# The opening of a decoder block's input projection: three plain units on un-normalised operands

## The chip, the core and the metric

The kernel runs on one core of one Trainium2 chip. The core has five engines with a queue each: TensorE (PE; its weight loads, PEld, run beside its matmuls), VectorE (DVE), ScalarE (ACT), GpSimd (POOL) and SyncE (SP), which here issues all DMAs. The metric is the time of one execution in microseconds on the device; lower is better.

## What is computed

One layer of a decoder with two mixers side by side. Sequence 2048, model width 1024, all in float32.

```
h    = rmsnorm(x, norm1_g)                  # per position: x / rms(x) * gain
proj = h @ w_in                             # 1024 -> 3088: q, k, v, g, a, conv B, C, H
o    = rmsnorm(gla(q, k, v, a)) * silu(g)   # gated linear attention, 4 heads, chunked
conv = B * causal_conv3(C * H)
x    = x + concat(o, conv) @ w_out
h2   = rmsnorm(x, norm2_g)
x    = x + (silu(h2 @ w_gate) * (h2 @ w_up)) @ w_down
return rmsnorm(x, norm_f_g)
```

The change touches the first two lines: the norm of x, and the first columns of the projection (k, q and half of v).

## The kernel before

**Products in three passes.** A float32 operand is split into a high and a low part: ACT copies it to the matmul's reduced format (L163), DVE subtracts that from the original (L164). A product is three matmuls of 128x128 by 128x512: high by high, and high by low both ways.

**Blocks and units.** The 2048 positions are four blocks of 512, j = 0..3; a half is two blocks. Activations lie with features on the partitions: x of one block is eight slices of 128 features, k = 0..7 (input `xt`); `x` has the same numbers by rows. A unit is 256 output columns for a half, its weights four quarters of 128x512: A11, A12, A22, A21. The operands of a half are the quarters B11 (k 0 to 3, first block), B12 (k 0 to 3, second block), B21, B22 (k 4 to 7). A *plain* unit has all eight quarter products, 96 matmuls. Every other unit (`unit`) makes seven products of sums of quarters, 84 matmuls; the weights' sums S1 to S4 are made on POOL (L430 to L437), the operands' differences T1 to T4 for a half once, and each is then split. Its products are, in order, A11.B11, S1.T1, S2.T2, A12.B21, S3.T3, S4.B22, A22.T4.

**The opening.** Units 0 and 1 of half 0 are plain, 2 to 11 are not. `first_loads` loads the rows of block 0 in half rows, unit 0's weights, the rows of block 1 and the slices of block 1. ACT squares the rows with a running sum (L595, L565), and TensorE transposes the rows of block 0 into slices, 32 transposes (L599). `rows_rstd` (L540) makes the factor 1/rms of each position, spreads it over partitions by copies (L552) and turns it by four transposes (L555). `build_first` (L322) multiplies each slice by gain and factor (L615), splits it and gives it to unit 0 (L362 to L364), first all of block 0, then block 1. `plain_unit` (L385) is unit 1; the differences T1 to T4 are made from the normalised slices (L374).

**What sets the order.** Instructions are issued to the engines by a planner that takes them by priority, in the order in which they are written, as soon as its own clock finds them ready. `issue_after` puts an instruction behind another on its engine. Buffers limit how far ahead work may run: four weight buffers (`wqp`), 28 operand buffers (`opp`), eight banks of results, eleven work tiles ("b"). Beside the units runs a list of background steps; `tick` (L241), called after each product, takes one step, at each call while `hurry` is set and at every second one else. In half 0 it holds the gate's weights, a pause of 8 steps, the gate of half 0 (32 matmuls L702, four L724, then four forget gates in tile g) taken in turn with the squares of blocks 2 and 3 (`row_stats`, half rows), and `h1_ahead`, which makes the operands of half 1.

Of the kernel before, what the change touches and what calls it, by code (L numbers as in the profile page):

```python
# [10 lines left out]
F32 = mybir.dt.float32  # L11
# [41 lines left out]
def tile_hymba_block(ctx, tc, x, xt, win, wa, wgu, wout, wffn, wdown, wdown_first, small, out):  # L53
# [98 lines left out]
    second_weights, unit_splits, unsplit = [], [], []  # L152
# [8 lines left out]

    def split(src, hi, lo):
        last_hi[:] = [act.activation(hi, src, AF.Copy)]  # L163
        last_lo[:] = [dve.tensor_tensor(lo, src, hi.bitcast(F32), ALU.subtract)]  # L164
        return last_lo[0]
# [94 lines left out]

    def pause(n):
        for _ in range(n):
            yield
# [58 lines left out]
    def build_first(quad, w):  # L322


        ops = {b: [] for _, b in PRODUCTS}
        h, o = {}, {}
        quarters = ("A11", "A12"), ("A21", "A22")
        los = []

        def weight(n, i, *marks):  # L330
            with ExitStack() as stack:
                for m in (last_exp[0], *marks):
                    stack.enter_context(tc.issue_after(m.ins))
                w[n] = weight_quarter(first_raw[0][:, i, :])

        weight("A11", 0, last_copy[0])
        los.append(last_lo[0])
        for j in range(2):
            for r in range(2):
                o[r, j] = bank()  # L340
            for k in range(KD):
                with tc.issue_after(los[-2 if len(los) > 2 else -1].ins):
                    h[k, j] = quad(k, j)
                if (j, k) == (0, 0):
                    weight("A21", 3, last_scaled[0])
                x = opp.tile([P, 2, PB], F32R, name="op", tag="op")
                los.append(split(h[k, j][:], x[:, 0, :], x[:, 1, :]))
                hi = last_hi[0]
                if j == 0 and k in (1, 2):
                    weight(*(("A12", 1), ("A22", 2))[k - 1], los[-1])  # L350
# [5 lines left out]
                name = ("B11", "B12")[j] if k < 4 else ("B21", "B22")[j]  # L356
                ops.setdefault(name, []).append(x)
                c = slice(k % 4 * P, (k % 4 + 1) * P)
                for r in range(2):
                    q = w[quarters[r][k // 4]]  # L360
                    with tc.issue_after(last_turn[0].ins):
                        pe.matmul(o[r, j][:], q[:, 0, c], x[:, 0, :], start=k == 0, stop=False)  # L362
                    pe.matmul(o[r, j][:], q[:, 1, c], x[:, 0, :], start=False, stop=False)
                    pe.matmul(o[r, j][:], q[:, 0, c], x[:, 1, :], start=False, stop=k == KD - 1)  # L364

        def differences(wanted):
            for n, y, a, b in (
                ("T1", (0, 0), (0, 1), (0, 0)), ("T2", (0, 0), (4, 1), (0, 0)),
                ("T3", (0, 1), (4, 1), (0, 1)), ("T4", (0, 0), (4, 0), (0, 0)),
            ):  # L370
                for k in range(4 if n in wanted else 0):
                    yy, aa, bb = [h[k + dk, j] for dk, j in (y, a, b)]
                    with tc.issue_after(los[-1].ins):
                        dve.tensor_tensor(yy[:], aa[:], bb[:], ALU.subtract)  # L374
# [142 lines left out]
    def row_stats(b):  # L517
# [11 lines left out]
        for t in range(PT):  # L529
            xs = nxt  # L530
            if t + 1 < PT:
                nxt = fetch(t + 1)
# [855 lines left out]
```

## Time and profile before

| | |
|---|---|
| median of 3 runs | 2062.1 us (2059.88 to 2063.85) |
| span of the profiled execution | 2059.3 us |
| TensorE busy, of the span | 2018.4 us (98%) |
| DVE, ACT, POOL busy | 1425.3, 959.7, 859.8 us |
| first product of unit 0 starts | 16.39 us |
| granted TensorE clock, mean | 0.996 |

The span is from the first to the last instruction of one profiled execution; of that execution no other time is given, and the runs' times hold what lies around the span as well. Times in the profile count from the span's start. A busy TensorE is one that has a matmul in its pipeline. Rows in order of time give start, duration, engine, line, operation, output and inputs, shapes, and in brackets the idle time before them with what ended it. Rows by stretch give, for each engine, busy time and the number of instructions, then the granted clock, the busy share of the DMA engines and GB/s.

### The profile page before, as it was taken

What the parts mean: (1) busy time and instruction counts of PE and PEld (TensorE: products, weight loads), DVE (VectorE), ACT (ScalarE), POOL (GpSimd) and SP (SyncE); (2) the same over time, 40 slices, a digit from 0 to 9 for tenths busy, and PEclk for the clock granted to TensorE, in tenths of its full rate; (3) what the DMA queues carried; (4) which work ended last, traced back from release to release, by engine and by line L of the source; (5) the groups of instructions that cost most, each with busy time, mean ns of one, the idle gap of its engine ahead of it and who ended that gap; (6) DMA issues with size and microseconds to landing.
All of it is one profiled execution on the core that took longest, in us unless ns stands there. A gap on an engine that the chain in (4) does not pass through costs nothing.

```text
span 2059.3 us, 27063 instructions
## 1 busy us (share of the span) xinstructions
PE 2018.4 (98%) x9229; PEld 1657.3 (80%) x9229; DVE 1425.3 (69%) x2128; ACT 959.7 (47%) x1918; POOL 859.8 (42%) x622
## 2 busy tenths in 40 slices
PE   7999999999999999999999999999999999999997
PEld 6877888787888888888888878787888888878786
DVE  8789686559743886676675676767666666667774
ACT  6655365765542344444444452334434444453344
POOL 0345322122102564464564345534644544435544
PEclk9999999999999999999999999999999999999998
DMA  6378485416586873545454676476444434586653
GB/s 229 116 274 278 159 319 165 143 67 194 190 296 246 311 254 130 198 181 207 156 185 143 241 264 254 185 282 257 163 164 167 175 140 169 179 309 223 234 217 126
DMA packets 188729, 421.47 MB, mean 205 GB/s; under 512 B 19792, under 2 KB 65072, under 8 KB 178992
## 3 DMA queue, kind: packets, MB, share of 16 engines
q1 hardware_dynamic: 188592, 419.76, 57.2%
q8 instruction: 72, 1.18, 0.2%
q14 instruction: 65, 0.53, 0.1%
HBM read 274.98 MB, written 144.70 MB: 204 GB/s over the span
## 4 chain that ended last, share of the span: by engine, by line
PE 84%; DVE 7%; DMA 4%; ACT 3%; issue 1%; POOL 1%; SPq 0%; DVEq 0%; ACTq 0%; POOLq 0%
PE mm L448 24%; PE mm L449 23%; PE mm L450 23%; PE mm L945 3%; PE mm L948 3%; PE mm L946 3%; DVE wq L164 2%; DVE op L164 1%; DMA op<-sa_B 1%; DMA op<-sa_T 1%; PE a_ps L702 1%; ACT wq L163 1%; DMA siT<-lo 1%; PE o_ps L869 1%; PE o_ps L871 1%
## 5 line engine op out<-in xcount | busy, mean ns | idle before, releaser
L448 PE MATMUL mm<-op,wq 128*128 128x512 f32 x2499 | 973.7, 392 | 10.3 <-ACT c L480 5.3
L449 PE MATMUL mm<-op,wq 128*128 128x512 f32 x2499 | 972.5, 390 | 1.6 <-DVE op L164 1.6
L450 PE MATMUL mm<-op,wq 128*128 128x512 f32 x2499 | 961.3, 390 | 2.6 <-DVE wq L164 2.3
L164 DVE TENSOR_TENSOR wq<-raw,wq 128x512 fp32r<-128x512 f32 (+2 forms) x626 | 508.9, 818 | 262.6 <-ACT wq L163 260.0
L163 ACT ACTIVATE wq<-raw 128x512 fp32r<-128x512 f32 (+2 forms) x626 | 364.9, 589 | 585.6 <-PE mm L450 447.9
L448 PEld LDWEIGHTS mm<-op,wq 128*128 128x128 f32 x2499 | 468.9, 188 | 114.9 <-ACT c L480 8.0
L450 PEld LDWEIGHTS mm<-op,wq 128*128 128x128 f32 x2499 | 469.1, 188 | 103.8 <-DVE wq L164 6.1
L449 PEld LDWEIGHTS mm<-op,wq 128*128 128x128 f32 x2499 | 469.3, 188 | 99.1 <-DVE op L164 3.7
L432 POOL TENSOR_TENSOR raw<-s,raw 128x512 f32<-128x512 f32 (+2 forms) x97 | 133.3, 1374 | 518.5 <-DVE wq L164 474.7
L430 POOL TENSOR_TENSOR s<-raw 128x512 f32<-128x512 f32 (+2 forms) x97 | 127.4, 1313 | 247.5 <-DMA raw<-in_wffn_dram 90.7
L473 DVE TENSOR_TENSOR c<-mm,c 128x512 f32<-128x512 f32 x198 | 135.8, 686 | 72.7 <-PE mm L450 70.9
L473 DVE TENSOR_TENSOR y<-mm,y 128x512 f32<-128x512 f32 x185 | 126.9, 687 | 83.3 <-PE mm L450 82.9
L437 POOL TENSOR_TENSOR raw<-raw 128x512 f32<-128x512 f32 (+2 forms) x97 | 120.6, 1244 | 126.7 <-DVE wq L164 126.7
L927 POOL TENSOR_TENSOR ssx<-ssx,q 128x512 f32<-128x512 f32 x52 | 77.4, 1504 | 158.8 <-ACT q L926 158.5
L431 POOL TENSOR_TENSOR raw<-raw 128x512 f32<-128x512 f32 (+2 forms) x97 | 137.3, 1416 | 4.9
L480 ACT ACTIVATE c<-mm 128x512 f32<-128x512 f32 x198 | 116.1, 587 | 11.1 <-PE mm L450 9.3
L945 PE MATMUL mm<-op,wq 128*128 128x512 f32 x256 | 100.9, 395 | 0.0
L946 PE MATMUL mm<-op,wq 128*128 128x512 f32 x256 | 99.7, 389 | 0.0
L163 ACT ACTIVATE wq<-s 128x512 fp32r<-128x512 f32 (+2 forms) x97 | 56.9, 587 | 89.3 <-PE mm L450 85.4
L164 DVE TENSOR_TENSOR wq<-s,wq 128x512 fp32r<-128x512 f32 (+2 forms) x97 | 82.6, 852 | 2.8 <-ACT wq L163 2.1
L164 DVE TENSOR_TENSOR op<-op 128x512 fp32r<-128x512 f32 x94 | 76.8, 844 | 4.7 <-ACT op L163 4.6
L948 PE MATMUL mm<-op,wq 128*128 128x512 f32 x256 | 79.8, 390 | 0.0
(204 smaller groups left out, 1807.6 us busy)
## 6 DMA issues: line engine op xcount, KB each, us to landing
raw<-in_wffn_dram SPq DMA_DIRECT2D x44, 1024.0 KB, 6.5
sa_B<-so SPq DMA_DIRECT2D x47, 512.0 KB, 4.2
op<-sa_B SPq DMA_DIRECT2D x47, 512.0 KB, 7.1
raw<-in_win_dram SPq DMA_DIRECT2D x23, 1024.0 KB, 5.4
sa_T<-so SPq DMA_DIRECT2D x44, 512.0 KB, 4.5
op<-sa_T SPq DMA_DIRECT2D x44, 512.0 KB, 6.9
raw<-in_wdown_dram SPq DMA_DIRECT2D x24, 768.0 KB, 5.8
sx<-y SPq DMA_DIRECT2D x48, 256.0 KB, 4.0
```

The source lines that it names most:

```text
L163: last_hi[:] = [act.activation(hi, src, AF.Copy)]
L164: last_lo[:] = [dve.tensor_tensor(lo, src, hi.bitcast(F32), ALU.subtract)]
L430: pool.tensor_tensor(s1, a21, a22, ALU.add)
L431: pool.tensor_tensor(a21, a11, a21, ALU.subtract)
L432: pool.tensor_tensor(a11, s1, a11, ALU.subtract)
L448: pe.matmul(o[:], wh, xh, start=first and k == 0, stop=False, skip_group_check=True)
L449: pe.matmul(o[:], wh, xl, start=False, stop=False, skip_group_check=True)
L450: return pe.matmul(o[:], wl, xh, start=False, stop=k == n - 1, skip_group_check=True)
L473: dve.tensor_tensor(t[:], o[:], t[:], ALU.add)
L945: pe.matmul(o[e, j][:], wh, m[:, 0, :], start=k == 0, stop=False)
L946: pe.matmul(o[e, j][:], wh, m[:, 1, :], start=False, stop=False)
L948: pe.matmul(o[e, j][:], wl, ops[k][j][:, 0, :], start=False, stop=k == KD - 1)
```

## The change

Block 0's slices are loaded from `xt` and no longer transposed. The first three units are plain, and their operands are slices with the gain alone; the factor of a position is multiplied onto their results (`out`). The normalised slices (`normed`), B11 to B22 and T1 to T4, serve unit 3 and those after it. All rows, those of blocks 2 and 3 too, are squared in the opening. Twelve matmuls on a tile of ones come first. From there to the weights of unit 3 each ACT and each DVE instruction is put behind the one written before it (`queued`); a low part is held back until the next high part has been issued (`late`, `catch_up`). TensorE's first turn lies behind its product of column (1, 1), its second turn behind the first quarter of unit 1, and the products that follow lie behind the turns. `between` puts the last operands and results among unit 3's weights. The gate is a background step without pause or squares.

Of the diff, its core; inside `opening` the removed lines that a line-by-line comparison puts between the new ones are left out.

```diff
-    second_weights, unit_splits, unsplit = [], [], []
+    unit_splits, unsplit = [], []
...
+    tails, late, ordered = {}, [], []
+
+    def queued(eng, issue):
+
+        with behind([tails[eng]] if eng in tails else []):
+            tails[eng] = issue()
+        return tails[eng]
+
+    def catch_up():
+        while late:
+            last_lo[:] = [queued(dve, late.pop(0))]
+
+    def split_in_order(src, hi, lo, gain=None):
+
+        scale = 1.0 if gain is None else gain
+        last_hi[:] = [queued(act, lambda: act.activation(hi, src, AF.Copy, scale=scale))]
+        catch_up()
+        top = hi.bitcast(F32)
+        if gain is None:
+            late.append(lambda: dve.tensor_tensor(lo, src, top, ALU.subtract))
+        else:
+            late.append(
+                lambda: dve.scalar_tensor_tensor(lo, src, gain, top, ALU.mult, ALU.subtract)
+            )
+
     def split(src, hi, lo):
+        if ordered:
+            return split_in_order(src, hi, lo)
         last_hi[:] = [act.activation(hi, src, AF.Copy)]
         last_lo[:] = [dve.tensor_tensor(lo, src, hi.bitcast(F32), ALU.subtract)]
         return last_lo[0]
...
-    def in_turn(one, *others):
-
-        for other in others:
-            for _ in other:
-                yield
-                if next(one, True) is None:
-                    yield
-        yield from one
-
...
-    def build_first(quad, w):
-
...
-                if j == 0 and k < PT:
-                    with tc.issue_after(hi.ins):
-                        row_squares(k)
-                if (j, k) == (0, PT + 2):
-                    rbs[1] = rows_rstd(squares[1][:, :, 0])
...
-    def plain_unit(src, ops, differences):
-
-        raw = raw_weights(src)
-        us, columns = [], (("B11", "B21"), ("B12", "B22"))
-        w = [weight_quarter(raw[:, i, :]) for i in (0, 1, 3, 2)]
-        second_weights[:] = last_hi + last_lo
-        differences(("T1", "T2", "T3"))
...
-    def unit_weights(src, raw=None):
+    def unit_weights(src, raw=None, between=()):
         raw = raw_weights(src) if raw is None else raw
+        between = iter(between)
+
+        def others():
+            for job in next(between, ()):
+                job()
+
...
         w["S1"] = weight_quarter(s1)
+        others()
         w["S2"] = weight_quarter(a11)
+        others()
         w["A12"] = weight_quarter(a12)
+        others()
         w["S3"] = weight_quarter(a21)
+        others()
         pool.tensor_tensor(a12, a12, a11, ALU.subtract)
         w["S4"] = weight_quarter(a12)
+        others()
         w["A22"] = weight_quarter(a22)
+        others()
         halves.clear()
         return w
 
...
-    def unit(src, ops, into=None, onto=None, raw=None):
-
-
-
-        w = unit_weights(src, raw)
+    def unit(src, ops, into=None, onto=None, raw=None, between=()):
+
+
...
-    def row_stats(b):
-        ssq = mtiny.tile([P, PT, 2], F32, name="ssq", tag="ssq")
-
...
+    def opening():
...
+        warm = bank("warm")
+        for _ in range(12):
+            pe.matmul(warm[:, 0:P], ones[:], ones[:], start=True, stop=True)
+        for what, i in (
+            (fetch_w, 0), (fetch_x, (0, 0)), (fetch_w, 3), (fetch_x, (1, 0)), (fetch_x, (2, 0)),
+            (fetch_w, 1), (fetch_rows, (0, 0)), (fetch_x, (3, 0)), (fetch_w, 2),
+            (fetch_x, (4, 0)), (fetch_rows, (0, 1)), (fetch_x, (5, 0)), (fetch_rows, (0, 2)),
+            (fetch_x, (6, 0)), (fetch_x, (7, 0)), (fetch_x, (0, 1)), (fetch_rows, (0, 3)),
+        ):
+            what(*i) if isinstance(i, tuple) else what(i)
+        for k in range(1, KD):
+            fetch_x(k, 1)
+        raws = {1: raw_weights(win[1])}
         for t in range(PT):
+            fetch_rows(1, t)
+        ordered.append(True)
...
+        def operand(k, j):
+            x = raw_op[k, j] = opp.tile([P, 2, PB], F32R, name="op", tag="op")
+            split_in_order(h[k, j][:], x[:, 0, :], x[:, 1, :], col(C_G1 + k))
+        def square(b, t):
+            if b not in squares:
+                squares[b] = mtiny.tile([P, PT, 2], F32, name="ssq", tag="ssq")
+            r = rows[b, t][:]
+            queued(
+                act,
+                lambda: act.activation(
+                    r, r, AF.Square, accum_out=squares[b][:, t, 0:1]
+                ),
+            )
+        def first_estimate(b):
+            v, l, y = [mtiny.tile([P, PT], F32, name=n, tag=n) for n in ("msq", "rl", "ry")]
+            ssq = squares[b][:, :, 0]
+            queued(
+                dve, lambda: dve.tensor_scalar(v[:], ssq, 1.0 / D, EPS, ALU.mult, ALU.add)
+            )
+            queued(act, lambda: act.activation(l[:], v[:], AF.Ln))
+            queued(act, lambda: act.activation(y[:], l[:], AF.Exp, scale=-0.5))
+            return v, l, y
+        def spread(v, l, y):
+            for f in (
+                lambda: dve.tensor_tensor(l[:], y[:], y[:], ALU.mult),
+                lambda: dve.scalar_tensor_tensor(l[:], l[:], -0.5, v[:], ALU.mult, ALU.mult),
+                lambda: dve.scalar_tensor_tensor(v[:], l[:], 1.5, y[:], ALU.add, ALU.mult),
+            ):
+                queued(dve, f)
+            rep = bt("rep", (P, PT, P))
             for t in range(PT):
+                queued(
+                    dve,
+                    lambda: dve.tensor_copy(
+                        rep[:, t, :], v[:, t : t + 1].to_broadcast([P, P])
...
+        def turn(rep, mark):
+            rb = bank("rb_ps")
+            with behind([mark]):
+                for t in range(PT):
+                    done = pe.transpose(rb[:, t * P : (t + 1) * P], rep[:, t, :], ident[:])
+            return rb, done
+        def keep(b, rb):
+            rbs[b] = bt("rb")
+            queued(act, lambda: act.activation(rbs[b][:], rb[:], AF.Copy))
+        def normed(k, j, rb):
+            y = h[k, j][:]
+            queued(
+                dve,
+                lambda: dve.scalar_tensor_tensor(
+                    y, y, col(C_G1 + k), rb[:], ALU.mult, ALU.mult
+                ),
+            )
+        def out(o, dst, j, r):
+            c = tt("c")
+            queued(dve, lambda: dve.tensor_tensor(c[:], o[:], rbs[j][:], ALU.mult))
+            store(dst[0][j][dst[1] + r][:], c[:])
+        def difference(y, a, b):
...
+        def made(n):
+            for k in range(4):
+                b11, b12, b21, b22 = h[k, 0], h[k, 1], h[k + 4, 0], h[k + 4, 1]
+                y, a, b = {
+                    "B11": (b11, None, None), "B21": (b21, None, None), "B22": (b22, None, None),
+                    "T1": (b11, b12, b11), "T2": (b11, b22, b11), "T3": (b12, b22, b12),
+                    "T4": (b11, b21, b11),
+                }[n]
+                if a is not None:
+                    difference(y, a, b)
+                final(n, k, y)
...
+        def column(k, j):
+            for r in range(2):
+                if k == 0:
+                    o[0, r, j] = bank()
+                q = w[(("A11", "A12"), ("A21", "A22"))[r][k // 4]]
+                last = step3(o[0, r, j], q, k, raw_op[k, j], k == 0, k == KD - 1)
+            return last
...
+        def second(u, j, i):
+            for r in range(2):
+                if i == 0:
+                    o[u, r, j] = bank()
+                q = w[(("A11", "A12"), ("A21", "A22"))[r][i]]
+                for k in range(4 * i, 4 * i + 4):
+                    last = step3(o[u, r, j], q, k, raw_op[k, j], k == 0, k == KD - 1)
+            return last
+        def outs(u, j):
+            for r in range(2):
+                out(o[u, r, j], ((s_kq, 0), (s_kq, 2), (s_v, 0))[u], j, r)
...
+        weight("A11", w_raw[:, 0, :])
+        operand(0, 0)
+        weight("A21", w_raw[:, 3, :])
+        operand(1, 0)
+        operand(2, 0)
+        weight("A12", w_raw[:, 1, :])
+        square(0, 0)
+        operand(3, 0)
+        weight("A22", w_raw[:, 2, :])
+        operand(4, 0)
+        square(0, 1)
+        operand(5, 0)
+        square(0, 2)
+        operand(6, 0)
+        operand(7, 0)
+        operand(0, 1)
+        square(0, 3)
+        catch_up()
+        for k in range(KD):
+            column(k, 0)
+        est = first_estimate(0)
+        operand(1, 1)
+        operand(2, 1)
+        rep = spread(*est)
+        catch_up()
+        for k in range(2):
+            mark = column(k, 1)
+        rb0, turned = turn(rep, mark)
+        for k in range(3, KD):
+            operand(k, 1)
+        catch_up()
+        with behind([turned]):
+            for k in range(2, KD):
+                column(k, 1)
+        weights(1, "A11", "A21")
+        catch_up()
+        keep(0, rb0)
+        for k in range(KD):
+            normed(k, 0, rb0)
+        outs(0, 0)
         for t in range(PT):
+            square(1, t)
+        weights(1, "A12", "A22")
+        for t in range(PT):
+            fetch_rows(2, t)
+        est = first_estimate(1)
+        made("B11")
+        catch_up()
+        rep = spread(*est)
+        rb1, turned = turn(rep, second(1, 0, 0))
+        keep(1, rb1)
+        with behind([turned]):
+            for j, i in ((0, 1), (1, 0), (1, 1)):
+                second(1, j, i)
+        for t in range(PT):
+            square(2, t)
+        raws[2] = raw_weights(win[2])
+        for i in range(6):
+            load(
+                carry[16 * i : 16 * i + 16, 0:2, :],
+                wgu[0:16, :].rearrange("p (h c) -> p h c", c=P),
+            )
+        for t in range(PT):
+            fetch_rows(3, t)
         for k in range(KD):
+            normed(k, 1, rb1)
+        outs(0, 1)
+        made("T1")
+        catch_up()
+        outs(1, 0)
+        weights(2, "A11", "A21")
+        catch_up()
+        for t in range(PT):
+            square(3, t)
+        second(2, 0, 0)
+        weights(2, "A12", "A22")
+        catch_up()
+        outs(1, 1)
+        raw3 = raw_weights(win[3])
+        made("T2")
+        catch_up()
+        for j, i in ((0, 1), (1, 0), (1, 1)):
+            second(2, j, i)
+        made("B21")
+        catch_up()
+        outs(2, 0)
+        made("T3")
+        between = [
+            [],
+            [partial(made, "B22"), partial(outs, 2, 1)],
+            [partial(made, "T4")],
+        ]
+        return ops, raw3, between
...
-    ops, first, differences = build_h()
+    ops, raw, between = opening()
     hurry.append(True)
     background.extend(
         [
-            gate_weights(), pause(8), in_turn(gate(0, ops), row_stats(2), row_stats(3)),
-            unhurried(),
-            h1_ahead(),
+            gate_weights(), gate(0, ops), unhurried(), h1_ahead(),
         ]
     )
-    in_proj(0, ops, first, differences)
+    in_proj(0, ops, raw, between)
     drain_background(lambda: len(background) < 2)
```

More of the change, by code (lines that the diff above doesn't have):

```diff
@@ L2 @@
 from collections import deque
+from functools import partial
 from itertools import chain
@@ L627, in gate_weights @@
         r0, r1 = raw[:, 0:4, 0:16], raw[:, 4:8, 0:16]
-        with behind(second_weights):
+        with behind(unit_splits):
             split(r0, top[:, :, 2, :], top[:, :, 3, :])
```

235 lines of the change are left out of this document (69 added, 166 removed).

## The prediction

> **What bounds the kernel now.** I read the page first, then busy time by stretch, the groups of the first 28 us, and the first 45 us in order of time.
>
> ```profile
> span 2059.3 us, 27063 instructions
> PE 2018.4 (98%) x9229; PEld 1657.3 (80%) x9229; DVE 1425.3 (69%) x2128; ACT 959.7 (47%) x1918; POOL 859.8 (42%) x622
> ...
> PE 84%; DVE 7%; DMA 4%; ACT 3%; issue 1%; POOL 1%; SPq 0%; DVEq 0%; ACTq 0%; POOLq 0%
> ```
>
> TensorE sets the time: it is busy for 98% of the span and holds 84% of the chain that ended last. A change of the opening pays only by what it moves the point at which TensorE has done a given piece of work.
>
> ```profile
> core 0: us, PE busy (x) PEld busy (x) DVE busy (x) ACT busy (x) POOL busy (x), PEclk, DMA share, GB/s
> 0.00:28.30 28.30, 17.06 (x75) 13.96 (x76) 19.27 (x47) 18.98 (x42) 1.11 (x7) 0.94 0.88 315
> 28.30:61.00 32.70, 32.70 (x147) 27.10 (x146) 31.46 (x52) 18.72 (x36) 9.80 (x3) 1.00 0.36 130
> 61.00:110.30 49.30, 49.30 (x218) 40.55 (x217) 34.72 (x66) 32.76 (x74) 13.44 (x9) 1.00 0.40 138
> 110.30:160.00 49.70, 48.43 (x214) 38.69 (x212) 39.44 (x70) 25.64 (x51) 27.83 (x19) 1.00 0.81 284
> 160.00:200.00 40.00, 37.78 (x165) 30.96 (x166) 37.67 (x44) 20.48 (x41) 23.97 (x16) 1.00 0.84 283
> ```
>
> ```profile
> L362 PE MATMUL mm<-op,wq 128*128 128x512 f32 x12 | 5.5, 458 | 2.4 <-ACT op L163 2.4
> L363 PE MATMUL mm<-op,wq 128*128 128x512 f32 x12 | 5.4, 447 | 0.0
> L364 PE MATMUL mm<-op,wq 128*128 128x512 f32 x12 | 4.2, 431 | 0.0
> ```
>
> The first fence is busy time by stretch, the second the TensorE groups of the first 28.3 us. By 28.3 us only 36 products of unit 0 have been started. From there to 110.3 us TensorE has no gap: 147 + 218 entries, less two counted on both sides of a border and three transposes, are 360 products in 82.0 us, 0.228 us each. So the 396 products of units 0 to 3 with the gate (96 + 96 + 84 + 84, and 32 + 4) are through at 110.3 us. I chose this mark because the new kernel has the same work there, plus 12 products.
>
> **The change, step by step.** These are rows of the opening in order of time (start, duration, engine; rows between them are left out).
>
> ```profile
> 4.96 0.63 ACT L595 ACTIVATE q<-xr 128x512 f32<-128x512 f32 x1 [2.89 <-DMA xr<-in_x_dram]
> 7.33 0.63 ACT L595 ACTIVATE q<-xr 128x512 f32<-128x512 f32 x1 [0.94 <-DMA xr<-in_x_dram]
> ...
> 12.75 0.16 DVE L177 SCALAR_TENSOR_TENSOR msq<-rl,ry 128x4 f32<-128x4 f32 x1
> ...
> 16.24 1.04 ACT L565 ACTIVATE xr<-xr 128x1024 f32<-128x1024 f32 x1
> 16.39 0.73 PE L362 MATMUL mm<-op,wq 128*128 128x512 f32 x1 [2.42 <-ACT op L163]
> 16.92 0.63 PE L363 MATMUL mm<-op,wq 128*128 128x512 f32 x1
> 17.18 0.19 ACT L565 ACTIVATION_READ_ACCUMULATOR xr<-xr 128x1 f32 x1
> 17.34 0.63 PE L362 MATMUL mm<-op,wq 128*128 128x512 f32 x1
> ...
> 24.07 0.19 ACT L169 ACTIVATE rl<-msq 128x4 f32<-128x4 f32 x1
> 24.29 0.21 ACT L170 ACTIVATE ry<-rl 128x4 f32<-128x4 f32 x1
> 26.11 0.63 ACT L163 ACTIVATE op<-h 128x512 fp32r<-128x512 f32 x1 [0.62 <-DVE h L615]
> 27.58 0.63 DVE L552 COPY rep<-msq 128x128 f32<-128x128 f32 x4
> 28.35 0.48 PE L362 MATMUL mm<-op,wq 128*128 128x512 f32 x1
> 30.77 1.29 POOL L430 TENSOR_TENSOR s<-raw 128x512 f32<-128x512 f32 x1 [28.96 <-DMA wa<-in_wa_dram]
> 31.35 1.27 DVE L164 TENSOR_TENSOR op<-h,op 128x512 fp32r<-128x512 f32 x1
> 34.24 0.73 DVE L615 SCALAR_TENSOR_TENSOR h<-h,sml,rb_ps 128x512 f32<-128x512 f32 x1
> 34.90 0.68 DVE L164 TENSOR_TENSOR op<-h,op 128x512 fp32r<-128x512 f32 x1
> 35.50 0.74 DVE L615 SCALAR_TENSOR_TENSOR h<-h,sml,rb_ps 128x512 f32<-128x512 f32 x1
> ```
>
> Prices: a two-tensor DVE operation over 512 columns takes its place for 0.60 us (34.90 to 35.50), one with a column factor for 0.66 (34.24 to 34.90), a tiny one 0.16 (12.75), taken as 0.2 since each waits for the one before, the four copies that spread the factors 0.63. On ACT a high part costs 0.63, the logarithm and exponential 0.43 together, a square over 1024 columns 1.04 plus 0.19 for its sum.
>
> *Loads.* Two fine windows give the rate.
>
> ```profile
> 10.00:15.00 5.00, 1.98 (x16) 1.48 (x14) 3.28 (x13) 4.42 (x13) 0.00 (x0) 1.00 1.05 408
> 15.00:20.00 5.00, 3.62 (x9) 2.84 (x10) 4.86 (x8) 3.92 (x8) 0.00 (x0) 0.66 1.03 397
> ```
>
> The first piece of 256 KB is there at 4.96, the third at 7.33; from then on about 400 GB/s, or 0.65 us per piece. In the new order the last slice of the first column, x(7,0), is byte 4.72 million and lands at 7.33 + 3.93/0.40 = 17.2; the last rows of block 0 (5.50 million) at 19.1; unit 1's weights (8.39 million) at 26.3. Block 0's slices are 2 MB more than before, 5.2 us of loading, and SP's queue carries the rows between them: without the 1.57 MB of rows ahead of it x(7,0) would land 3.9 us sooner. Both lie in these landings.
>
> *TensorE until the first turn.* It no longer waits for a normalised operand (16.39 now), nor has it the 32 transposes of x. The second piece lands at about 5.7 (4.96 and 0.65), their high parts 0.63 later: first product near 6.4. The twelve warming products are not in the old trace; they cost nothing while they end by then: from about 1, at most 0.42 each as the slowest products quoted, they end by 6.1. It then follows the slices: x(7,0) at 17.2, its parts 18.5, its products 19.5.
>
> *The ordered DVE queue.* ACT squares the last rows from 19.1 to 20.3; the mean 0.2, logarithm and exponential 0.4: 21.0; high part of x(1,1) 21.6. From there DVE works without a break in the written order: low part of x(1,1) 0.66; three tiny steps and four copies 1.2 (23.5); six low parts 4.0 (27.5); unit 1's A11 and A21 1.2 (28.7); eight norms 5.3 (34.0); two results of unit 0 1.2 (35.2); A12, the mean, A22 1.4, with 0.6 of waiting for ACT (37.2); four low parts of B11 2.4 (39.6); three tiny steps and four copies 1.2: 40.9. A11 and A21 can only be split when unit 0's buffer is free: TensorE has column 1 through k = 3 at 19.5 + 1.4, wait to 22.3, 1.0, transposes to 23.9, 2.7: 26.7; its high part is ready at 27.4, just in time.
>
> *The wait that takes the old one's place.* TensorE ends unit 0 at 26.7 + 5.5 = 32.2 and unit 1's first quarter at 37.7. Everything behind it is tied to the second turn, which needs the copies of 40.9. It stands about 3 us and goes on at 41.0 (the row at 28.35 stands 0.14 behind the copies' end). All else of unit 1 is queued behind it.
>
> *From 41.0 on* there are 72 + 96 + 84 products: 57.4 us, to 98.4; the gate's 36 add 8.2: 106.6. The 12 extra products of the third plain unit (2.7 us) are in this. The nearest cover: unit 2's first weights come on DVE after 41.1 + 5.3 (norms) + 1.2 + 4.8 (T1) + 1.2 + 1.2 = 54.8, wanted at 57.4. S3 comes behind S2, which waits for POOL and a buffer until about 78.6, then 0.6 + 2.4 (B22) + 1.2 + 0.6 + 4.8 (T4) + 0.6 = 88.8, wanted at 79.3 + 4 x 2.73 = 90.2. The extra DVE work (12 results, which ACT copied before, and 12 low parts of B11, B21, B22, 14.4 in all) is hidden only there; its uncovered part is the 3 us.
>
> So 110.3 - 106.6 = **3.7 us gained in the opening**. Bounds: without the wait 3 more; if the loads keep the 0.65 us pace from the first on, 1.1 more (the third piece was that late); with TensorE at half clock 2.6 less (below).
>
> *Behind the opening.* The 16 half-row squares of blocks 2 and 3 leave the background.
>
> ```profile
> PE mm L450 <- DVE wq L164: 1.8, 4, 0.6
> PE mm L448 <- ACT c L480: 1.7, 1, 1.7
> ```
>
> These are TensorE's waits from 110 to 260 us, 3.5 in all, where DVE is busy 37.67 of 40 with blocks 2 and 3's operands. That work can start sooner, with its squares and buffers ready. Ends: all 3.5 gone, or a new wait as in the second rival below; I take 1.0 gone, nearer to nothing, as the DVE and POOL work itself stays.
>
> The sum: -3.7 - 1.0 = -4.7 on the profiled span (2059.3), carried over to the runs' median of 2062.1: **2057.4**. A measurement tells about 0.2% (4.1 us) from no change, so the forecast lies just beyond that.
>
> **Rivals.** *Half clock in the opening, so that the early start buys little.* At 16.92 to 17.34 products stand 0.42 us apart, and the clock is 0.66 in the window from 15, after one in which TensorE was busy 1.98 of 5 us. If the twelve warming products don't hold the clock up and it is half until 19.9 as here, 32 products are done by then; the 40 left to column 1, k = 3, with the turn, end at 29.5, A11's parts wait until 30.2 and the queue slips 2.6: 2060.0. Against: by the landings TensorE's new gaps before 18.5 are short ones, some 3.5 us in 12.
>
> The Trainium skill (TensorE: Matmul & The Clock Gate, Part 1) says that the clock drops to half when a free-running window of about 3.4 us passes idle, and comes back after a busy one. The trace agrees: the half clock follows the emptiest stretch, the two windows quoted with the loads. By that rule the 3 us wait at the second turn would just not drop it; were it over 3.4, one window at 0.42 would lose 1.6 us: 2059.0.
>
> *The gate crowds unit 4.* The pause and the squares between the gate's steps are gone, so all four forget gates are issued within unit 3.
>
> ```profile
> 85.00:114.00 29.00, 15.28 (x28) 9.24 (x20) 1.00 0.61 212
> ```
>
> This row is their tile g on DVE and ACT: 15.3 us on DVE, spread over 29. DVE from 79.2: B22 2.4, two results 1.2, A12 0.6, T4 4.8, S3, S4, A22 1.8, unit 3's sums 1.8, the gate 15.3, unit 4's A11 and S1 1.2, and four POOL sums that each stretch a DVE operation by 0.6 (1.27 at 31.35): 31.5, to 110.7, against 106.6. The wait of 4.1 gives 2062.1 - 3.7 + 4.1 = 2062.5. For it: priority follows the order of issue. Against: the gate waits on ACT in between, and TensorE now loses nothing while it runs (49.30 busy of 49.30).
>
> The Trainium skill (SBUF — State Buffer, SBUF: two separate sides) has POOL and a DVE operation with two SBUF inputs hold a shared port by turns for a whole instruction. The row at 31.35 agrees: 1.27 where 0.68 is usual (34.90). If each of the four held DVE for its full 1.29, the sum would be 2.8 larger: 2065.3.
>
> *Slower.* The same place, with the factors of blocks 2 and 3 ahead of unit 4's weights too, their squares being ready. One set has thirteen tiny steps, 2.6, and its copies:
>
> ```profile
> 124.45 1.74 DVE L552 COPY rep<-ry 128x128 f32<-128x128 f32 x4
> ```
>
> That is 4.3 per set: the wait is 8.4 with one, 12.7 with both: 2066.8 to 2071.1. It decides from a wait of 7.8 on. For it: DVE is the opening's bound already. Against: unit 4's weights can slip in while tiny steps wait.
>
> **How the numbers follow.** The forecast's case 0.60, with a range of its own from 2053 to 2059.5; about 0.50 of it lies below 2058.0 and 0.10 above. Half clock 0.08 and the crowded unit 4 0.14 end within 0.2%; the slower case has 0.18. That makes faster 0.50, same 0.32, slower 0.18. The range: below, 2057.4 less 1.1 of loads, less the 2.5 left of the later waits, less 1.3 of the 3 us wait: 2052.5; above to the slower case's near end, 2066.5.
>
> **What would show it.** First product near 6.4 and clock 1.00 until 20; last square of block 0 at about 20; DVE without gaps from 21.6 to 40.9; one TensorE wait of about 3 us on the second turn near 38; unit 1's end at 57.4, the gate and unit 3 through at 106.6. Wrong would be the forecast if TensorE waits on DVE in units 2 to 4, if the slices land later than 17.2, or if the waits behind 110 grow.

## The result, and the profile after

The changed kernel takes 2070.3 us (median of 5 runs, 2067.6 to 2075.2) against 2061.3 for the kernel before on the same chip (5 runs, 2059.3 to 2063.9): a ratio of 1.0046, 95% interval 1.0033 to 1.0059, so 9 us slower. Forecast was 2057.4 from 2062.1. The profiled execution is the slowest of the five (2075.2), 5 us above the median; the opening is read from it all the same.

The page of the changed kernel:

```profile
span 2073.3 us, 27045 instructions
...
PE 2027.9 (98%) x9233; PEld 1665.2 (80%) x9233; DVE 1429.2 (69%) x2139; ACT 955.8 (46%) x1891; POOL 845.5 (41%) x618
...
PE 83%; DVE 9%; DMA 3%; ACT 3%; issue 2%; SPq 1%; POOL 0%; DVEq 0%; ACTq 0%; POOLq 0%
```

TensorE is the bound as before, but DVE holds 9% of the chain instead of 7%. Busy time of TensorE by stretch (length, busy time with its entries, granted clock, DMA share, GB/s):

```profile
0.00:28.30 28.30, 23.34 (x98) 0.94 0.92 330
28.30:61.00 32.70, 30.26 (x129) 0.95 0.76 284
61.00:110.30 49.30, 44.16 (x186) 0.93 0.24 86
110.30:160.00 49.70, 47.19 (x204) 0.97 0.59 199
160.00:200.00 40.00, 39.72 (x174) 1.00 0.92 322
```

The start is earlier (23.34 us busy by 28.3 instead of 17.06), but the two stretches that were full before, 147 and 218 entries at clock 1.00, hold 129 and 186 at 0.95 and 0.93. TensorE's groups up to 110.3 us, the mark of the prediction:

```profile
L630 PE MATMUL mm<-op,wq 128*128 128x512 f32 x96 | 38.8, 409 | 3.8 <-ACT op L178 3.8
L631 PE MATMUL mm<-op,wq 128*128 128x512 f32 x96 | 38.4, 402 | 0.0
L632 PE MATMUL mm<-op,wq 128*128 128x512 f32 x96 | 36.4, 398 | 0.0
L396 PE MATMUL mm<-op,wq 128*128 128x512 f32 x20 | 8.9, 446 | 5.1 <-ACT wq L178 5.1
...
L831 PE MATMUL a_ps<-op,wa_sb 128*128 128x512 f32 x30 | 7.1, 394 | 0.0
```

That is 288 + 3 x 20 + 30 = 378 of the 408 products of units 0 to 3 with the gate. The 30 missing ones are 6.8 us at 0.228: in this execution the opening is 6.8 us slower, not 3.7 faster. Part of that is this execution's own: phase, a run below with the same opening, has 390 products by the mark (4.1 us behind), and it kept full clock from 15 to 20 and from 40 to 45 us, where this one shows 0.68 and 0.71. Where the time goes, in order of time:

```profile
21.04 1.06 ACT L546 ACTIVATE xr<-xr 128x1024 f32<-128x1024 f32 x1 [0.26 <-DMA xr<-in_x_dram]
39.45 0.39 PE L632 MATMUL mm<-op,wq 128*128 128x512 f32 x1
41.90 0.63 DVE L573 COPY rep<-msq 128x128 f32<-128x128 f32 x4
42.27 1.08 PE L583 MATMUL rb_ps<-ident,rep 128*128 128x128 f32 x4 [2.44 <-DVE rep L573]
...
90.31 0.39 PE L398 MATMUL mm<-op,wq 128*128 128x512 f32 x1
95.17 1.66 ACT L178 ACTIVATE wq<-raw 128x512 fp32r<-128x512 f32 x3
95.83 0.80 PE L396 MATMUL mm<-op,wq 128*128 128x512 f32 x1 [5.13 <-ACT wq L178]
96.73 0.53 ACT L191 ACTIVATE wa_sb<-wa 128x64 fp32r<-128x64 f32 x3
112.28 0.68 DVE L844 TENSOR_TENSOR a_sb<-a_ps,a_sb 32x512 fp32r<-32x512 f32 x1 [7.29 <-ACT a_sb L843]
```

The wait at the second turn (39.45 to 42.27) was forecast. The one in unit 3 (90.31 to 95.83) was not: S3's high part comes at 95.17, and after S2 x T2 nothing else is ready, because the gate's weights (L191) come behind it and A12 x B21 stands behind the gate. These are the gate's 32 products, with first and last start, in the kernel before and in the changed one:

```profile
L702 PE MATMUL a_ps<-op,wa_sb x32: 391/394/400, 69.3 to 79.2; 128*128 128x512 f32 x32
L831 PE MATMUL a_ps<-op,wa_sb x32: 391/394/400, 103.4 to 110.6; 128*128 128x512 f32 x32
```

DVE stands 7.3 us until the gate's sums are there (112.28). In this execution each of the two waits is followed by half clock:

```profile
40.00:45.00 5.00, 2.73 (x9) 2.37 (x10) 3.40 (x12) 2.04 (x5) 0.00 (x0) 0.71 1.00 359
95.00:100.00 5.00, 4.17 (x10) 3.30 (x11) 4.01 (x10) 2.57 (x8) 0.00 (x0) 0.50 0.20 43
```

A second loss lies far behind the opening. The chain of additions there, in the kernel after and, below it, before:

```profile
474.30 0.39 PE L398 MATMUL mm<-op,wq 128*128 128x512 f32 x1
475.36 1.09 DVE L909 SCALAR_TENSOR_TENSOR c<-u,sml,c 128x512 f32<-128x512 f32 x1
475.97 1.59 POOL L373 TENSOR_TENSOR raw<-raw 128x512 f32<-128x512 f32 x1
476.37 1.75 DVE L903 TENSOR_TENSOR u<-c,c 128x512 f32<-128x512 f32 x1
478.04 0.68 DVE L424 TENSOR_TENSOR c<-mm,c 128x512 f32<-128x512 f32 x1
478.77 0.61 PE L396 MATMUL mm<-op,wq 128*128 128x512 f32 x1 [4.08 <-DVE c L424]
```

```profile
470.93 0.68 DVE L473 TENSOR_TENSOR c<-mm,c 128x512 f32<-128x512 f32 x1
471.53 1.17 DVE L780 TENSOR_TENSOR u<-c,c 128x512 f32<-128x512 f32 x1
```

Before, the addition that TensorE needs stood ahead of the product u; after, it stands behind it, and u is stretched to 1.75 beside a POOL sum. TensorE waits 4.1 us. That is the place of the other loss.

### The profile page after: what moved, and what is told of

It reads as the page before. It is cut to its first block, busy times and chain, and to the rows that moved or that the text cites. A ratio compares the mean times of both kernels' runs of the same rounds, so it can differ in the third digit from the quotient of the medians.

```text
span 2073.3 us, 27045 instructions
## 1 busy us (share of the span) xinstructions
PE 2027.9 (98%) x9233; PEld 1665.2 (80%) x9233; DVE 1429.2 (69%) x2139; ACT 955.8 (46%) x1891; POOL 845.5 (41%) x618
## 4 chain that ended last, share of the span: by engine, by line
PE 83%; DVE 9%; DMA 3%; ACT 3%; issue 2%; SPq 1%; POOL 0%; DVEq 0%; ACTq 0%; POOLq 0%
PE mm L396 23%; PE mm L398 23%; PE mm L397 23%; PE mm L1068 3%; PE mm L1071 3%; PE mm L1069 3%; DVE wq L192 2%; DVE op L192 1%; DMA op<-shT 1%; DMA op<-sa_T 1%; PE a_ps L831 1%; PE o_ps L992 1%; PE o_ps L994 1%; DVE op L182 1%; ACT wq L191 1%
## 5 line engine op out<-in xcount | busy, mean ns | idle before, releaser
L396 PE MATMUL mm<-op,wq 128*128 128x512 f32 x2439 | 953.7, 394 | 21.6 <-DVE c L424 6.9
L397 PE MATMUL mm<-op,wq 128*128 128x512 f32 x2439 | 952.1, 391 | 1.4 <-DVE op L192 1.3
L398 PE MATMUL mm<-op,wq 128*128 128x512 f32 x2439 | 940.0, 391 | 2.7 <-DVE wq L192 2.4
L192 DVE TENSOR_TENSOR wq<-raw,wq 128x512 fp32r<-128x512 f32 (+2 forms) x606 | 489.6, 813 | 243.8 <-ACT wq L191 241.2
L191 ACT ACTIVATE wq<-raw 128x512 fp32r<-128x512 f32 (+2 forms) x606 | 351.8, 586 | 562.4 <-PE mm L398 437.9
L396 PEld LDWEIGHTS mm<-op,wq 128*128 128x128 f32 x2439 | 459.3, 188 | 125.8 <-ACT c L431 9.0
L398 PEld LDWEIGHTS mm<-op,wq 128*128 128x128 f32 x2439 | 459.6, 188 | 101.7 <-DVE wq L192 5.0
L397 PEld LDWEIGHTS mm<-op,wq 128*128 128x128 f32 x2439 | 459.7, 188 | 96.1 <-DVE op L192 2.5
L374 POOL TENSOR_TENSOR raw<-s,raw 128x512 f32<-128x512 f32 (+2 forms) x96 | 124.6, 1298 | 523.4 <-DVE wq L192 476.6
L424 DVE TENSOR_TENSOR c<-mm,c 128x512 f32<-128x512 f32 x195 | 133.7, 686 | 78.6 <-PE mm L398 76.9
L424 DVE TENSOR_TENSOR y<-mm,y 128x512 f32<-128x512 f32 x185 | 126.9, 687 | 83.5 <-PE mm L398 82.9
L1068 PE MATMUL mm<-op,wq 128*128 128x512 f32 x256 | 101.1, 395 | 0.0
L191 ACT ACTIVATE wq<-s 128x512 fp32r<-128x512 f32 (+2 forms) x95 | 55.5, 584 | 96.8 <-PE mm L398 91.9
L1069 PE MATMUL mm<-op,wq 128*128 128x512 f32 x256 | 99.8, 390 | 0.0
L1071 PE MATMUL mm<-op,wq 128*128 128x512 f32 x256 | 79.8, 390 | 0.0
```

The costliest lines, as they stand in the source:

```text
L374: pool.tensor_tensor(a11, s1, a11, ALU.subtract)
L396: pe.matmul(o[:], wh, xh, start=first and k == 0, stop=False, skip_group_check=True)
L397: pe.matmul(o[:], wh, xl, start=False, stop=False, skip_group_check=True)
L398: return pe.matmul(o[:], wl, xh, start=False, stop=k == n - 1, skip_group_check=True)
L424: dve.tensor_tensor(t[:], o[:], t[:], ALU.add)
L1068: pe.matmul(o[e, j][:], wh, m[:, 0, :], start=k == 0, stop=False)
```

## The experiments

Differences in us are the difference of two ratios to the kernel before, times 2061. Each ratio's interval is about 0.001 (2 us) to either side, up to 0.002 in the slowest, so a difference of two ratios under some 3 us is not clear of noise by the times alone.

**The order inside unit 3.**

```diff
t4_late      between: -[T4 behind A12]  +[T4 behind A22]
gate_later   -gate_weights(), gate(0, ops)   +gate_weights(), pause(2), gate(0, ops)
turn_first   -est; made("B11"); catch_up(); spread(*est)
             +est; catch_up(); spread(*est); made("B11"); catch_up()
all3         the three together
```

> The four differences T4 with their high and low parts are issued behind S4 and A22 instead of behind A12; nothing else is moved. Theory (the loss sits in unit 3, where S3's high part comes behind T4 on the ordered queues): TensorE's wait of 5.3 us at 90.3 and the half clock behind it (about 2 us) go, the gate and unit 3 are through at about 110 us instead of 117, time about 2063.5 against 2070.3 for the changed kernel. Rival (the added work on DVE or the 12 added products are the loss, wherever S3 stands): S4 or A22's T4 is late instead, through still at 115 to 117, time 2068 to 2071.

> Two empty steps ahead of the gate in the background, so that the bank of A12 x B21 is asked for before those of the gate; A12 x B21 then stands ahead of S3 x T3 on TensorE, as it did in the kernel before. Theory (the place of A12 x B21 was the cover that went): its 2.7 us fall into the 5.3 us wait, the rest of 2.6 stays, and the half clock behind it is shorter or as long: 2.7 to 4 us less, 2066.5 to 2067.5. Rival (A12's parts come too late to be a cover, or the gate's new place costs as much): within 1 us of 2070.3.

> The spreading of block 1's factor is issued ahead of B11's parts on DVE. The second turn comes 2.4 to 2.6 us sooner (39.8 instead of 42.3), and without the wait the half clock at 42 to 45 goes: units 1 and 2 end about 4 us sooner. Theory (S3's place on the ordered queue sets unit 3): S3 is only 1.2 sooner, so the wait in unit 3 grows to about 8 us and the time falls by 1 to 2 us, to about 2069. Rival (the two waits add up independently): 4 to 4.5 us less, about 2066.

> The three edits together. Theory: the wait at the second turn (2.6 and some 1.7 of half clock) and the one in unit 3 (5.3 and 2) both go: gate and unit 3 are through at 105 to 107 us, time 2058.5 to 2060, below the kernel before by 1 to 3 us. Rival (work behind the opening, not the waits, is the loss): through at 106 as well, but the waits behind 110 us grow and the time stays above 2064.

Measured: t4_late 2071.9 (ratio 1.0053), gate_later 2068.4 (1.0033), turn_first 2067.9 (1.0025), all3 2069.9 (1.0040). TensorE's waits of t4_late from 60 to 160 us:

```profile
PE mm L396 <- ACT op L178: 2.9, 1, 2.9
PE z L856 <- DVE a_sb L847: 2.0, 1, 2.0
PE mm L396 <- DVE c L424: 1.3, 1, 1.3
```

S3's wait is gone, and T4's parts and the gate's own steps are late instead. The first theory, that S3's place on the ordered queues is the loss, falls: moving one piece of DVE's work moves the wait. In gate_later the wait in unit 3 is 1.4 us; the two empty steps bring A12 x B21 back ahead of S3 x T3 (the last product ahead of the wait starts at 92.58 us instead of 90.31), and 2.7 us are gained, which alone is not clear of noise. So part of the cover did go with the pause that the diff removed. turn_first removes the wait at the second turn and its half clock whole; the stretch, and TensorE's only wait from 28 to 110 us:

```profile
28.30:61.00 32.70, 32.70 (x148) 27.06 (x147) 32.31 (x70) 22.10 (x42) 3.00 (x2) 1.00 0.79 282
```

```profile
PE mm L396 <- ACT wq L178: 5.5, 1, 5.5
```

There are 148 entries where the changed kernel has 129, and 135 in phase, which kept full clock: 3.0 to 4.3 us. The wait in unit 3 is hardly longer (5.5, where my theory had 8), and the time falls by 4.3, so the two waits do add up, against my theory. all3 misses its forecast of 2058.5 to 2060 by ten and shows what the others hide: without the waits TensorE runs into DVE at 93 us (3.6 us) and into the gate's steps (3.2).

**The counter.** Between products of a unit, every second count hands a step to the background. The kernel before has 22 counts by the end of unit 3 (8 in unit 1, 7 each in units 2 and 3; the 18 below is a miscount, but even as well). The changed one has 7, since the plain units of the opening count no more.

```diff
-    pace, ahead, hurry = [0], [], []
+    pace, ahead, hurry = [1], [], []
```

> The counter that lets every second product of a unit hand over to the background starts at 1 instead of 0, so that the counts are as even as in the kernel before at the same product. Theory (the kernel before had 18 such counts by the end of unit 3, the changed one has 7; the odd number shifts the steps of the second half's forget gate by one product, and the sum c is late for product 1788): the wait of 4.2 us at 474 us with its half clock (1.8) goes, about 4.5 us less in all, 2065 to 2066.5; the opening stays as it is. Rival (the wait at 474 follows from the lateness of the opening): it stays, 2069 to 2071.

Measured: 2066.9 (1.0026), 4.1 less. Its waits from 400 to 700 us have instead of the 4.1 at L424:

```profile
PE sc L968 <- DVE kq L958: 1.3, 1, 1.3
PE v_ps L977 <- ACT carry L984: 1.2, 1, 1.2
PE sc L968 <- PE mm L1071: 0.4, 1, 0.4
PE mm L396 <- DVE c L424: 0.3, 1, 0.3
```

The 1.3 is one that the kernel before has at the same place (474 us). The opening keeps its two waits (2.7 and 4.0 us). The loss at 474 follows from the odd count, not from the opening: gate_mid, below, has the wait too (4.1 us), though its opening is early.

**The steps of blocks 2 and 3's factors.**

```diff
 def rows_rstd(ssq, rb):
-        dve.tensor_scalar(v[:], ssq, 1.0 / D, EPS, ALU.mult, ALU.add)
+        with behind(unit_splits):
+            dve.tensor_scalar(v[:], ssq, 1.0 / D, EPS, ALU.mult, ALU.add)
```

combo is this with turn_first and gate_later; combo_phase has the counter at 1 as well.

> The tiny DVE steps that turn the squares of blocks 2 and 3 into factors are issued behind the last weight parts of unit 3; nothing else is moved. Theory (the ordered DVE queue is the bound from the second turn to the end of unit 3, and these 24 steps with 3.7 us in it, at 48 to 67 us, make S3 late): S3 comes 3 to 4 us sooner, TensorE's wait in unit 3 falls from 5.3 to about 2, time 2065.5 to 2067.5 against 2070.3. Rival (the steps fit into DVE's gaps, or they cost as much where they go): within 1.5 us of 2070.3.

> Second turn ahead of B11, gate two steps later, the factors of blocks 2 and 3 behind unit 3's weights. Theory (DVE's queue): no wait of TensorE over 1 us between 40 and 105 us, gate and unit 3 through at 105 to 107 us, the wait at 474 still there: 2061 to 2063. Rival (the later place of the factors only moves the loss to unit 4): through at 107 too, but 4 us or more of new waits between 110 and 170 us, 2065 to 2068.

> The same, with the counter starting at 1. Theory: 4.5 us less than without, 2056.5 to 2059, below the kernel before. Rival: no difference between the two.

Measured: 2077.6 (1.0074), 2076.8 (1.0069) and 2076.1 (1.0064): 4 to 6 us worse than the changed kernel, and all three theories are missed by 10 to 17 us. In rstd_late the wait in unit 3 falls to 3.0 from 5.1 (4.0 in phase), as it should, but from 110 to 200 us stands

```profile
PE mm L396 <- ACT c L431: 4.8, 2, 4.4
PE mm L396 <- DVE c L424: 3.1, 1, 3.1
PE mm L398 <- DVE wq L192: 1.1, 1, 1.1
```

The tiny steps now lie among unit 4's sums and the forget gates. The rival holds: in the opening these steps cost 1 to 2 us, in unit 4 more. This is the place and mechanism of the slower rival of the prediction; the changed kernel escapes it, because the planner runs these steps at 52 to 73 us. combo_phase is only 1 us better than combo, as its rival had it: the wait at 474 goes, but TensorE is busy 4.0 us less between 110 and 300 us (174.33 instead of 178.36). What the counter is worth depends on what else is moved.

**The gate's place.** In the changed kernel the six small parts of the gate's weights (the text of gw_early says nine) are tied behind unit 3's last weight parts (`unit_splits`), where the kernel before tied them behind unit 1's (`second_weights`).

```diff
gw_early      -        with behind(unit_splits):      (no tie)
joined        gw_early + turn_first + phase
joined_rows   joined, rows (0, 0..2) loaded and squared behind x(4,0), x(5,0), x(6,0)
joined_pause  joined + pause(2)
```

> The nine small parts of the gate's weights are no longer tied behind the last weight parts of unit 3; nothing else is moved. The gate's 32 products then stand ahead of S2 x T2 on TensorE, and its steps on DVE start sooner. Theory (in the changed kernel the gate has to wait for unit 3's last parts at 95 us, so its 7.3 us of TensorE work can't fill the wait in unit 3, and DVE idles for it at 101 to 108 us and is crowded after): the wait of 5.3 us at 90 and its half clock go, gate and unit 3 through at 110 to 111 us instead of 117, time 2062.5 to 2064.5 (the wait at 474 stays). Rival (DVE's whole work to 145 us is the bound, wherever the gate stands): the loss comes back in unit 4, time 2067 or more.

> Second turn ahead of B11, the gate's weights untied, the counter starting at 1. Theory: the gains of the three add up, since the gate now fills what the earlier second turn opens in unit 3: 7 (unit 3) + 4 (second turn) + 3.8 (counter) off 2070.3, 2055 to 2057.5, below the kernel before by some 5 us. Rival (unit 4 takes it back): 2060 to 2063.

> The three edits joined (second turn ahead of B11, the gate's weights untied, the counter starting at 1), and the first rows of block 0 (loads and squares) one or two places later, behind x(4,0). Theory: with no wait left behind 19 us the gap of 1.5 us before x(3,0) sits on TensorE's path, and 1 us of it goes: 2054 to 2056.5. Rival (the rows, not the slices, set the first turn and with it unit 1): the same time as without, or 0.5 us more.

> The three edits joined, with the two empty steps ahead of the gate, so that A12 x B21 stands among S2 x T2 and the gate's second part behind it. Theory (DVE's queue decides, and the gate's early start relieves it): the gate's steps start 2 to 3 us later on DVE, time 0 to 1.5 us above the three alone. Rival (the cover by A12 x B21 is worth its own 2.7 us even so): 1 to 3 us below them.

Measured: 2072.4 (1.0054), 2071.5 (1.0041), 2070.4 (1.0039), 2066.5 (1.0018). The first three miss their theories by 8 to 14 us. Untying let the parts run too far ahead: ACT stands 5.9 us on their load in gw_early, which also waits 4.6 us at 123 us for DVE's weight parts, as its rival had it. joined_pause, a row of ACT in order of time and TensorE's longest wait from 28 to 110 us:

```profile
53.08 0.55 ACT L191 ACTIVATE wa_sb<-wa 128x64 fp32r<-128x64 f32 x3 [8.08 <-DMA wa<-in_wa_dram]
```

```profile
PE mm L634 <- ACT wq L178: 4.4, 1, 4.4
```

ACT stands 8 us on the load of the gate's weights, unit 2's weight parts are queued behind it, and TensorE waits 4.4 us for them. But unit 3 has no wait any more. So the tie was moved, not taken away:

```diff
 gate_weights:   -with behind(unit_splits):   +with behind(gate_after):
 opening:         weights(2, "A12", "A22"); catch_up()
                 +gate_after[:] = last_hi + last_lo
gate_mid       this and pause(2)
tied_only      this alone
tied_no_turn   gate_mid + phase
tied           gate_mid + phase + turn_first
tied_rows      tied, with the rows as in joined_rows
```

> Two empty steps ahead of the gate, and the gate's weight parts tied behind unit 2's last weight parts instead of unit 3's; second turn and counter as in the changed kernel. Theory (the gate's place is the loss of the opening): the gate's 32 products and A12 x B21 stand ahead of S3 x T3, no wait of TensorE over 1 us between 45 and 110, gate and unit 3 through at about 110 us; 6 to 7 us off 2070.3, 2063 to 2064.5. Rival (DVE's work is the bound wherever the gate stands): 2066.5 or more, with the waits moved to 120 to 170 us.

> The gate's weight parts tied behind unit 2's last weight parts, and nothing else. The gate's 32 products then stand among A11 x B11 and S1 x T1, A12 x B21 behind S4 x B22. Theory (the tie alone is the cause, since 7.3 us of the gate's products fill the 5.3 us wait): as gate_mid, gate and unit 3 through at 109 to 112 us, 2063 to 2065.5. Rival (A12 x B21's bank is needed too): TensorE waits for S4 or for the gate's own steps, 2067 or more.

> As tied, with the second turn where the changed kernel has it. Theory (waits on the path add up once unit 3 no longer hides them): the wait of 2.6 to 2.9 us at 39 is all there, 2.5 to 4.5 us above tied's 2057.1: 2059.5 to 2061.5. Rival (DVE's queue absorbs it behind 110 us): within 1 us of tied.

> As gate_mid, with the second turn ahead of B11 and the counter starting at 1. Theory: the wait of 4.5 us at 55 us that joined_pause had, and its half clock, go: gate and unit 3 through at 105 to 106 us, time 2059.5 to 2061.5, level with the kernel before or 1 to 2 us below. Rival: DVE is crowded behind 110 us, 2063 to 2066.

> As tied, with the first rows of block 0 one or two places later. Theory: TensorE is bound from 18 us on, so the shorter gap before x(3,0) is kept: 1 to 1.5 us below tied, 2058.5 to 2060. Rival: no difference.

Measured: gate_mid 2064.9 (1.0014, 1.0005 to 1.0023), tied_only 2068.7 (1.0029), tied_no_turn 2060.7 (0.9992, 0.9982 to 1.0001), tied 2057.1 (0.9981, 0.9970 to 0.9991), tied_rows 2057.0 (0.9978, 0.9969 to 0.9988). gate_mid by stretch, and its only wait from 28 to 110 us:

```profile
61.00:110.30 49.30, 49.30 (x218) 40.56 (x217) 42.88 (x78) 27.71 (x54) 10.85 (x8) 1.00 0.29 96
```

```profile
PE rb_ps L587 <- DVE rep L577: 2.7, 1, 2.7
```

Unit 3 is full again, 218 entries as before the change, and the gate's products lie within it:

```profile
L836 PE MATMUL a_ps<-op,wa_sb x32: 391/394/400, 85.7 to 97.9; 128*128 128x512 f32 x32
```

By 110.3 us gate_mid has 422 products, 14 beyond the 408: its opening is 3.2 us ahead of the kernel before, where 3.7 were forecast. The gate's place is worth 6.6 us, the theory's 6 to 7. tied_only has a nearly full unit 3 too (waits of 0.2 us) but gains only 3.5: at 120 us it waits 4.7 us on DVE's weight parts, so the bank of A12 x B21 seems to be needed too. The counter adds 4.5 (gate_mid to tied_no_turn), the second turn 2.3 more (to tied), which alone is not clear of noise. tied lands 2.4 below its own forecast. The rows' place makes no difference that can be told (tied_rows). tied, by groups up to 110.3 us and by its page:

```profile
L401 PE MATMUL mm<-op,wq 128*128 128x512 f32 x36 | 14.0, 390 | 0.0
L400 PE MATMUL mm<-op,wq 128*128 128x512 f32 x36 | 13.9, 390 | 0.0
L402 PE MATMUL mm<-op,wq 128*128 128x512 f32 x35 | 13.3, 390 | 0.0
L837 PE MATMUL a_ps<-op,wa_sb 128*128 128x512 f32 x32 | 7.7, 394 | 0.0
...
L859 PE MATMUL z<-a_sb,wgu_sb 96*128 96x512 f32 x4 | 1.3, 395 | 0.0
```

```profile
span 2053.1 us, 27061 instructions
...
PE 2020.0 (98%) x9233; PEld 1658.8 (81%) x9233; DVE 1432.6 (70%) x2139; ACT 961.0 (47%) x1896; POOL 847.3 (41%) x618
```

With the 288 of the plain units that is 431 products by 110.3 us: 23 beyond the 408, 5.2 us ahead of the kernel before and 53 products, 12 us, ahead of the changed one. DVE's last parts for unit 3 come only 3.5 us sooner than in the changed kernel (92.4 against 95.9 us); TensorE has the gate and A12 x B21 to do meanwhile. Some of the 5.2 is given back behind 110 us; by the times 3.9 are left (1.9 to 6.2). tied beats both kernels.

## Why the prediction was wrong, point by point

- **The extra products, the earlier start, the wait at the second turn: right in kind.** The first product starts at 6.77 (6.4 forecast), the wait is 2.8 us (3), and the three plain units cost no more than their products.
- **Landings and the ordered DVE queue: right in mechanism, mis-sized by 1.6 to 1.9.** The last square of block 0 starts at 21.04 instead of 19.1, the copies of the second factor end at 42.53 instead of 40.9. The 0.65 us per piece held only from about 10 us on (408 GB/s from 10 to 15 us, 134 to 366 in the slices from 2.3 to 9.8 us).
- **"It stands about 3 us and goes on at 41.0": the clock was taken as safe.** Here the row of 40 to 45 us shows 0.71: five products stood 0.43 us apart, 1.1 us. With the later copies, unit 2 ends some 3 us after the 79.3 forecast. But of the nine traces that have this wait, 2.8 to 3.1 us long, only five dropped the clock behind it. The forecast "clock 1.00 until 20" failed in this execution as well: behind a gap of 2.9 us at 11.4 the row of 15 to 20 us shows 0.68, while phase has 1.00 there.
- **The step that failed: "From 41.0 on there are 72 + 96 + 84 products ... the gate's 36 add 8.2: 106.6", with S3 at 88.8 "wanted at 90.2".** I took the gate's products as able to stand anywhere and A12 x B21 as standing ahead of S3. Both were in the diff: the tie of the gate's weights went from unit 1's parts to unit 3's, and the pause that kept the gate's banks behind A12 x B21 was taken out. I had used that pause only for DVE's share in unit 4. The gate's products came at 103.4 to 110.6 us instead, behind unit 3's wait. gate_mid puts both back in kind (a tie behind unit 2's parts, a pause of two steps) and gains 6.6; its opening stands 3.2 us ahead, near the 3.7 forecast.
- **S3 itself came at 95.2, not 88.8.** 1.6 of it is the later queue. In the rest lie the tiny steps of blocks 2 and 3, which I had costed behind unit 3 (1 to 2 us by rstd_late), and DVE operations stretched beside POOL sums; how much these have was not measured by itself.
- **"Behind the opening: 1.0 gone": wrong.** The counter's parity cost 4.1 there (phase), and the waits themselves did not shrink (4.7 us from 110 to 300 in tied_no_turn, 3.5 in the kernel before). The prediction doesn't name this step at all; `tick` stood in the code of `plain_unit` that the diff removes.
- **The slower rival** named 2066.8 to 2071.1, and the time fell into it, but by another mechanism: rstd_late, which does put the factors into unit 4, is slower still. **The crowded unit 4** was partly right: DVE stands 7.3 us for the late gate and is crowded after (43.86 us busy from 110.3 to 160, 39.44 before).
- **The sum.** From the changed kernel to tied: 6.6 (gate) + 4.5 (counter) + 2.3 (second turn) = 13.4 us. Without the last, which the forecast held as its 3 us wait, tied_no_turn is 1.6 faster than before (between 3.7 faster and 0.2 slower) where 4.7 were forecast; of the 3.1 between, 1.6 fits the later queue and 1.0 the later waits that didn't shrink, but with intervals of 2 us that is a reckoning, not a measurement.

## What to carry to other kernels

When a change rewrites the start of a schedule, list every tie, pause and counter that it removes or renames, and ask of each what it kept apart or together far behind: here three such lines cost 11 us, and with the tie and the pause put back in kind the new opening stood 3.2 us ahead of the old one, near what its arithmetic had promised. Work that can run anywhere (a gate's products) is the cover of whatever comes late; whoever ties it behind the late thing loses it twice, as cover and as the start of its own chain. And taking a tie away is not moving it: an untied instruction can stand at the head of an in-order queue and wait for a load.

## What the runs showed of the hardware

A wait of TensorE of 2.4 us can drop its clock to half. I counted pauses between starts of its matmuls, from 20 to 700 us of all 19 traces, and whether the clock record shows half clock behind, with at least five products 0.4 us or more apart: 2 of 46 pauses from 1.2 to 2.3 us, 18 of 25 from 2.3 to 3.45 (one drop stands behind a pause of each of these two kinds), 26 of 27 longer ones; a drop costs 1.1 to 1.7 us behind the middle ones, 1.4 to 3.0 behind the long ones. By the traces' clock record each of these stretches at half clock lasts 3.4 or 6.8 us. The same wait doesn't always do it. The changed kernel's at 39.45 us (2.8 us) did, with clock 0.71 in the window quoted above; gate_mid's at the same place, 3.1 us long, didn't:

```profile
40.00:45.00 5.00, 3.83 (x19) 3.29 (x20) 3.85 (x12) 3.15 (x6) 0.00 (x0) 1.00 1.01 399
```

The Trainium skill (TensorE: Matmul & The Clock Gate, Part 1) has the clock drop after at least one idle window of about 3.4 us, and the windows run freely. That the outcome depends on where the wait falls agrees; that a whole window must be idle does not, since 18 of the 25 waits of 2.3 to 3.45 us, all about a window long or shorter, dropped it. The measurement decides: from about 2.4 us on, half clock is to be reckoned with.
